# Half of the decay masks, one convolution tap and a scaling move to ScalarE in an FFN, SSD and convolution block

## The chip, the cores and the metric

The kernel runs as one program on one core of a Trainium2 chip. The metric is device time in microseconds (us). The time before is 1519.1 us, the median of three runs (1518.18 to 1520.67).

## The reference

One layer for 512 tokens of 1024 features, all in float32. Cut to what the change touches:

```python
x = x + 0.5 * swiglu(rms_norm(x, ffn1_norm), ffn1_w_in, ffn1_w_out)
h = rms_norm(x, mix_norm)
b_gate, c_gate, xa, z, xbc, dt_raw, ga, gb = split(h @ w_in)
y_a = (b_gate * causal_dwconv(c_gate * xa, short_conv_w)) @ short_w_out

xbc = silu(causal_dwconv(xbc, ssm_conv_w) + ssm_conv_b)        # 4 taps, bias
xs, bm, cm = split(xbc)                                        # 32 heads of 64; 8 groups of 128
dt = softplus(dt_raw + ssm_dt_bias);  a = -exp(ssm_A_log) * dt
decay = exp(segsum(a))               # exp of the sums of a over (s, l] within a chunk
y_diag = (C B^T * decay) @ (xs * dt) # within a chunk; y_off comes from the states before it
y_ssm = y_diag + y_off + xs * ssm_D
yf = y_ssm * silu(z)
y_b = (yf * rsqrt(mean over the group(yf^2) + eps) * ssm_norm) @ ssm_w_out

x = x + (sigmoid(ga) * y_a + sigmoid(gb) * y_b) @ w_out
x = x + 0.5 * swiglu(rms_norm(x, ffn2_norm), ffn2_w_in, ffn2_w_out)
out = rms_norm(x, final_norm)
```

## The kernel before

Features lie on the 128 partitions and the 512 tokens along the free axis. A float32 product is made of three float32r matmuls: weight and activation are each split into a high and a low part, and high times high, high times low and low times high are accumulated in one PSUM bank (L164 to L166). Each 128x1024 block of weights is loaded by SyncE (L121) into one of two `wraw` buffers, cast on ScalarE into `wh` (L125), and the rest `wl` is formed on VectorE (L126); `wh` and `wl` have three buffers each, so that a block is made ready two blocks ahead of its use.

TensorE's order is written by hand. `Order` counts ticks, a tick for every K-tile (three matmuls) of the main stream of projections; work that depends on other engines is put in so many ticks later with `sq.at`. The other engines' instructions are put in order by the scheduler of the framework, and each engine then runs its list in that order: an instruction that waits holds all behind it.

The mixer's SSD part goes over 8 groups of 4 heads, and each over 4 chunks of 128 tokens (`NC`). For a group, TensorE projects C, B and two tiles of x; each projection goes through `conv_silu`: `xp` is the scaled projection (VectorE, L372), `cv` starts as the tap of the present token (VectorE, L374), the three other taps are added (VectorE, L376), and ScalarE adds the bias and takes the SiLU (L378) into `cb` (C and B) or `xsT` (x). `inner` (L409) multiplies C and B. `x_tokens` turns x to tokens on partitions (`tr`, copied to `xt` by ScalarE, L431) and scales it into `xdd` (L437) and `xdt` (L440). For a chunk c, `steps` makes the masked decay steps `au`, two tiles of 128x512 in the high part `ah` and the low part `al` of a (GpSimd, L471), with three buffers; `weights` sums them on TensorE into the bank `sg` (two buffers, L480), ScalarE takes the exp into `ex` (L483), and VectorE masks it with `cbm` (L484); `within` (L493) multiplies by `xdt` into the bank `py`, and VectorE adds to `y` (L497, L498). `states` (L453) puts its product in the bank `po`, one buffer, which ScalarE (L458, first chunk) or VectorE (L460 and L463) reads before the next one may start. `skip` (L445) starts `y` on GpSimd. `gated` multiplies by the gate `zs`, squares and sums on ScalarE (L520), VectorE and GpSimd make the scale `rg` (L525, L527), and four VectorE instructions scale `y` (L529). `out` transposes y (L537) and ScalarE copies it to `yk` (L539). Group g's late steps run on TensorE among the projections of group g + 1, and for groups 1 to 7 the gate's products (L311 to L313) stand between the last x projection and the next group's.

Of the kernel before, what the change touches and what calls it, by code (L numbers as in the profile page):

```python
# [17 lines left out]
P = 128  # L18
# [14 lines left out]
# columns of the packed per-feature parameters  # L33
# [8 lines left out]
class Order:  # L42
    """The order of the tensor engine's work: the main stream advances in ticks (a K-tile of a
    projection each); what depends on other engines is put in so many ticks later."""
# [25 lines left out]
def hybrid_block(ctx: ExitStack, tc: tile.TileContext, xT, w1i, w1o, wmx, wz0, wso, wsso,  # L70
# [39 lines left out]
    def prep():  # L110
        """The next block of weights as two float32r parts whose sum is exact."""
# [46 lines left out]
    def mm3(out, w, xs, first=True, last=True, tk=slice(0, T)):  # L158
        """out += w.T @ x over the K-tiles xs, both in pairs of parts, for the tokens tk."""
# [19 lines left out]
    class Norm:  # L179
        """RMS norm of the residual: the parts of x * gain, and 1 / RMS per token, which the  # L180
        products are scaled by afterwards."""
# [119 lines left out]
    def gate(zw, wide, c0, cn):  # L301
        """z of a group for the token blocks c0 .. c0 + cn, tokens on the partitions."""
# [34 lines left out]
    def dt_chain():  # L337
        # softplus(v) = max(v, 0) + log1p(exp(-|v|)), log1p(e) = 2 atanh(e / (2 + e))
# [20 lines left out]
    def decays():  # L359
        """exp of the sums of a within a chunk: up to a token, after it, and of all."""  # L360
# [7 lines left out]
    def conv_silu(o, pt, ft):  # L368
        """Scale, causal convolution over 4 taps, bias and SiLU of one 128-channel tile."""
# [4 lines left out]
        nc.vector.tensor_scalar(cv, xp[:, 3:], col(PF_CW + 4 * ft + 3), None, ALU.mult)  # L374
# [3 lines left out]
        nc.scalar.activation(o, cv, AF.Silu, bias=col(PF_CB + ft))  # L378
# [7 lines left out]
    class Group:  # L386
        """One group of the SSD mixer: 4 heads that share B and C."""
# [10 lines left out]
        def heads(self, apx):  # L398
            """Values of the group's heads, each over its 64 channels."""
            n = apx.shape[1]  # L400
            return apx[:, :, self.hs].unsqueeze(3).broadcast_to([P, n, HG, HD])
# [356 lines left out]
```

## Time and profile before

| what | us |
| --- | --- |
| median of three runs | 1519.1 |
| the profiled execution: its span, first to last instruction | 1517.2 |
| around the span, by the median | 1.9 |
| TensorE busy | 1492.1 |
| VectorE busy | 830.2 |
| ScalarE busy | 533.9 |
| GpSimd busy | 267.3 |

The profiled execution has no time of its own besides its span; the 1.9 us are the median less the span. The first feed-forward runs to about 375 us, the SSD groups from there to about 760 us, then come the merge, the short convolution and the second feed-forward. A TensorE instruction's end is modelled and overlaps the next one's start, so that the start of one matmul to the start of the next tells its true cost: a projection's matmul is shown with 0.40 and the next starts 0.23 later.

### The profile page before, as it was taken

The page shows a single profiled execution, that of the slowest core. Times are in us where ns is not written, and L with a number is a line of the kernel's source. Part 1 is how long each engine was busy: PE and PEld are TensorE (multiplying, and loading weights), DVE is VectorE, ACT ScalarE, POOL GpSimd, SP SyncE. Part 2 cuts the span into 40 slices and gives each one's busy share as a digit, 9 for nine tenths or more (in the row PEclk, how much of TensorE's full clock was granted, in tenths as well). Part 3 has the DMA queues.
Part 4 walks back from the last instruction along what each step waited for, and adds up shares of the span by engine and source line. Part 5 has one row for each costly group of instructions (what it writes and reads, how often), then busy time and mean ns, then how long its engine had stood idle before and what let it go on. Part 6 is the DMA issues. An engine that isn't in the chain of part 4 may idle for free.

```text
span 1517.2 us, 17880 instructions
## 1 busy us (share of the span) xinstructions
PE 1492.1 (98%) x7214; PEld 1255.7 (83%) x7214; DVE 830.2 (55%) x990; ACT 533.9 (35%) x721; POOL 267.3 (18%) x236
## 2 busy tenths in 40 slices
PE   7999999999999999999999999999999999999997
PEld 6888888888878888888988888888888888888887
DVE  5545454323797877888754246654454545453223
ACT  5323222222455555445542122223243323232232
POOL 0111111000045442344300001111121111110011
PEclk9999999999999999999999999999999999999998
DMA  5333333323221221222222233333222222223233
GB/s 178 98 97 98 97 97 91 104 87 98 84 70 53 73 68 59 84 70 70 70 84 97 97 98 97 98 97 98 97 97 95 87 103 91 102 93 104 87 104 105
DMA packets 41539, 139.48 MB, mean 92 GB/s; under 512 B 4592, under 2 KB 7024, under 8 KB 41456
## 3 DMA queue, kind: packets, MB, share of 16 engines
q1 hardware_dynamic: 41456, 138.34, 28.7%
q8 instruction: 57, 0.93, 0.2%
q14 instruction: 26, 0.21, 0.0%
HBM read 136.22 MB, written 2.10 MB: 91 GB/s over the span
## 4 chain that ended last, share of the span: by engine, by line
PE 90%; DVE 5%; issue 3%; ACT 1%; DMA 0%; POOL 0%; SPq 0%; POOLq 0%; DVEq 0%; ACTq 0%
PE mm L166 27%; PE mm L164 27%; PE mm L165 27%; PE py L493 1%; PE mm L313 1%; PE mm L312 1%; PE mm L311 1%; DVE ex L484 1%; DVE wl L126 1%; PE po L504 1%; DVE xdd L437 1%; DVE cv L376 1%; PE sg L212 0%; ACT L483 0%; PE po L453 0%
## 5 line engine op out<-in xcount | busy, mean ns | idle before, releaser
L125 ACT CAST wh<-wraw 128x1024 fp32r<-128x1024 f32 (+3 forms) x261 | 269.6, 1033 | 715.9 <-PE mm L165 655.9
L164 PE MATMUL mm<-xw,wh 128*128 128x512 f32 x1256 | 503.2, 401 | 7.6 <-ACT wh L125 5.7
L126 DVE TENSOR_TENSOR wl<-wraw,wh 128x1024 fp32r<-128x1024 f32 (+3 forms) x261 | 394.2, 1511 | 199.7 <-ACT wh L125 198.5
L166 PE MATMUL mm<-xw,wl 128*128 128x512 f32 x1256 | 491.3, 391 | 0.3 <-DVE wl L126 0.3
L165 PE MATMUL mm<-xw,wh 128*128 128x512 f32 x1256 | 491.1, 391 | 0.0
L164 PEld LDWEIGHTS mm<-xw,wh 128*128 128x128 f32 x1256 | 237.0, 189 | 55.4 <-ACT wh L125 5.7
L166 PEld LDWEIGHTS mm<-xw,wl 128*128 128x128 f32 x1256 | 236.8, 189 | 51.6 <-DVE wl L126 1.4
L165 PEld LDWEIGHTS mm<-xw,wh 128*128 128x128 f32 x1256 | 237.2, 189 | 48.5 <-DVE xw L192 0.8
L164 PE MATMUL mm<-hk,wh 128*128 128x512 f32 (+1 forms) x374 | 141.1, 377 | 0.0
L165 PE MATMUL mm<-hk,wh 128*128 128x512 f32 (+1 forms) x374 | 140.8, 377 | 0.0
L166 PE MATMUL mm<-hk,wl 128*128 128x512 f32 (+1 forms) x374 | 140.8, 376 | 0.0
L250 POOL TENSOR_TENSOR hf<-sg,tu 128x512 f32<-128x512 f32 x44 | 58.6, 1331 | 401.9 <-ACT wh L125 343.2
L248 DVE TENSOR_TENSOR tu<-mm,rb 128x512 f32<-128x512 f32 x42 | 29.0, 691 | 134.6 <-PE mm L166 134.6
L165 PEld LDWEIGHTS mm<-hk,wh 128*128 128x128 f32 x374 | 70.4, 188 | 13.0
L164 PEld LDWEIGHTS mm<-hk,wh 128*128 128x128 f32 x374 | 70.4, 188 | 12.9
L166 PEld LDWEIGHTS mm<-hk,wl 128*128 128x128 f32 x374 | 70.4, 188 | 12.8
L376 DVE SCALAR_TENSOR_TENSOR cv<-xp,pf,cv 128x512 f32<-128x512 f32 x96 | 74.9, 780 | 1.2
L311 PE MATMUL mm<-wh,xw 128*128 128x256 f32 (+1 forms) x256 | 75.2, 294 | 0.0
L312 PE MATMUL mm<-wl,xw 128*128 128x256 f32 (+1 forms) x256 | 72.7, 284 | 0.0
L313 PE MATMUL mm<-wh,xw 128*128 128x256 f32 (+1 forms) x256 | 72.7, 284 | 0.0
L244 DVE TENSOR_TENSOR tg<-mm,rb 128x512 f32<-128x512 f32 x43 | 29.7, 691 | 67.8 <-PE mm L166 64.2
L203 POOL TENSOR_TENSOR nacc<-nacc,nsq 128x512 f32<-128x512 f32 x18 | 26.4, 1468 | 223.5 <-ACT nsq L201 223.5
(181 smaller groups left out, 1670.5 us busy)
## 6 DMA issues: line engine op xcount, KB each, us to landing
wraw<-wmx SPq DMA_DIRECT2D x86, 512.0 KB, 3.5
wraw<-w2i SPq DMA_DIRECT2D x44, 512.0 KB, 3.2
wraw<-w1i SPq DMA_DIRECT2D x43, 512.0 KB, 3.5
wraw<-w2o SPq DMA_DIRECT2D x18, 512.0 KB, 3.5
wraw<-w1o SPq DMA_DIRECT2D x16, 512.0 KB, 3.5
wraw<-wsso SPq DMA_DIRECT2D x16, 512.0 KB, 3.7
wraw<-wso SPq DMA_DIRECT2D x8, 512.0 KB, 3.2
wraw<-wmo SPq DMA_DIRECT2D x8, 512.0 KB, 3.3
```

What stands on the lines that cost most here:

```text
L125: nc.scalar.copy(wh[:, h], raw[:, h])
L126: nc.vector.tensor_tensor(wl[:, h], raw[:, h], wh[:, h].bitcast(F32), ALU.subtract)
L164: nc.tensor.matmul(out, wh[:, sl], xk[:, 0, tk], start=first and i == 0, stop=False)
L165: nc.tensor.matmul(out, wh[:, sl], xk[:, 1, tk], start=False, stop=False)
L166: nc.tensor.matmul(out, wl[:, sl], xk[:, 0, tk], start=False, stop=last and i == n - 1)
L244: nc.vector.tensor_tensor(tg, pg, nrm.rb, ALU.mult)
L248: nc.vector.tensor_tensor(tu, pu, nrm.rb, ALU.mult)
L250: nc.gpsimd.tensor_tensor(hf, sg, tu, ALU.mult)
L311: nc.tensor.matmul(o, xw[k][:, 0, tk], wh[:, sl], start=k == 0, stop=False)
L312: nc.tensor.matmul(o, xw[k][:, 0, tk], wl[:, sl], start=False, stop=False)
L313: nc.tensor.matmul(o, xw[k][:, 1, tk], wh[:, sl], start=False, stop=k == KT - 1)
L376: nc.vector.scalar_tensor_tensor(cv, xp[:, q : q + T], col(PF_CW + 4 * ft + q), cv, ALU.mult, ALU.add)
```

## The change

Four edits in the SSD part; the number of matmuls and the order of TensorE's and SyncE's instructions stay as they were.

- `steps`: the high half of the masked steps (`ah`) is no longer one GpSimd instruction of 128x512 but four ScalarE copies of 128x128, one a head, each with the head's value of a as a scale per partition. The low half stays on GpSimd.
- `conv_silu`: the first tap with the bias is a ScalarE instruction (Identity, with a scale and a bias per partition) in place of a VectorE one, and the SiLU no longer has a bias.
- `gated`: the four scalings of `y` by `rg` are ScalarE copies with a scale in place of VectorE instructions.
- Comments and docstrings are gone. Lines behind them move by at most 6: `ah` is L473, `al` L477, the exp L489, the first tap L374, the other taps L377, the SiLU L379, the scaling of `y` L535.

```diff
@@ -366,16 +366,17 @@
         nc.vector.tensor_tensor(dtd, dt, ds, ALU.mult)
 
     def conv_silu(o, pt, ft):
-        """Scale, causal convolution over 4 taps, bias and SiLU of one 128-channel tile."""
+
         xp = tp.tile([P, T + 3], F32, tag="ta", name="xp")
         nc.gpsimd.memset(xp[:, 0:3], 0.0)
         nc.vector.tensor_tensor(xp[:, 3:], pt, nm.rb, ALU.mult)
         cv = tp.tile([P, T], F32, tag="tb", name="cv")
-        nc.vector.tensor_scalar(cv, xp[:, 3:], col(PF_CW + 4 * ft + 3), None, ALU.mult)
+        nc.scalar.activation(cv, xp[:, 3:], AF.Identity, scale=col(PF_CW + 4 * ft + 3),
+                             bias=col(PF_CB + ft))
         for q in (2, 1, 0):
             nc.vector.scalar_tensor_tensor(cv, xp[:, q : q + T], col(PF_CW + 4 * ft + q), cv,
                                            ALU.mult, ALU.add)
-        nc.scalar.activation(o, cv, AF.Silu, bias=col(PF_CB + ft))
+        nc.scalar.activation(o, cv, AF.Silu)
 
     def hview(t, c0, c1):
         return t[:, c0:c1, :].rearrange("p c (h d) -> p c h d", d=HD)
...
@@ -464,17 +465,22 @@
             self.st[c + 1] = sn
 
         def steps(self, c):
-            """a of chunk c masked to the tokens up to l, [t, head, l], in two parts."""
+
             self.au[c] = []
-            for part in (ah.bitcast(F32), al):
-                au = tp.tile([P, HG, P], F32R, tag="td", name="au", bufs=3)
-                nc.gpsimd.tensor_tensor(
-                    au, tri.unsqueeze(1).broadcast_to([P, HG, P]),
-                    part[:, c, self.hs].unsqueeze(2).broadcast_to([P, HG, P]), ALU.mult)
-                self.au[c].append(au)
+            au = tp.tile([P, HG, P], F32R, tag="td", name="au", bufs=3)
+            for h in range(HG):
+                k = self.g * HG + h
+                nc.scalar.activation(au[:, h, :], tri, AF.Copy,
+                                     scale=ah.bitcast(F32)[:, c, k : k + 1])
+            self.au[c].append(au)
+            au = tp.tile([P, HG, P], F32R, tag="td", name="au", bufs=3)
+            nc.gpsimd.tensor_tensor(
+                au, tri.unsqueeze(1).broadcast_to([P, HG, P]),
+                al[:, c, self.hs].unsqueeze(2).broadcast_to([P, HG, P]), ALU.mult)
+            self.au[c].append(au)
 
         def weights(self, c):
-            """exp(sum of a over (s, l]) * C B^T of chunk c, [s, head, l]."""
+
             sgp = bank("sg")
             for i in range(2):
                 nc.tensor.matmul(sgp, mgt_r, self.au[c][i].rearrange("p h l -> p (h l)"),
...
@@ -526,8 +532,8 @@
             rg = tp.tile([P, NC], F32, tag="rg", name="rg")
             nc.gpsimd.tensor_tensor(rg, sm, nhalf, ALU.pow)
             for c in range(NC):
-                nc.vector.tensor_scalar(self.y[:, c, :], self.y[:, c, :], rg[:, c : c + 1], None,
-                                        ALU.mult)
+                nc.scalar.activation(self.y[:, c, :], self.y[:, c, :], AF.Copy,
+                                     scale=rg[:, c : c + 1])
 
         def out(self, i):
             if i == 0:
```

The scheduler puts ScalarE's, VectorE's and GpSimd's lists in another order. Three places follow. In these lists a row is a line, an operation, out<-in and a shape, `x4` stands for four in a row, and buffer numbers are left out except in the names of the states (`st_4661`).

GpSimd at the start of the mixer, group 0, from the scale `rt` of the norm on. Before:

```order
L217 TENSOR_TENSOR rt<-ms,nhalf 128x4
L371 MEMSET xp 128x3 x4
L471 TENSOR_TENSOR au<-cst,ah 128x512
L471 TENSOR_TENSOR au<-cst,al 128x512
L471 TENSOR_TENSOR au<-cst,ah 128x512
L371 MEMSET xp 128x3
L471 TENSOR_TENSOR au<-cst,al 128x512
L471 TENSOR_TENSOR au<-cst,ah 128x512
L445 TENSOR_TENSOR y<-xt,pr 128x1024
L471 TENSOR_TENSOR au<-cst,al 128x512
L471 TENSOR_TENSOR au<-cst,ah 128x512
```

The same stretch of GpSimd after:

```order
L217 TENSOR_TENSOR rt<-ms,nhalf 128x4
L371 MEMSET xp 128x3 x3
L477 TENSOR_TENSOR au<-cst,al 128x512
L371 MEMSET xp 128x3 x2
L446 TENSOR_TENSOR y<-xt,pr 128x1024
L477 TENSOR_TENSOR au<-cst,al 128x512 x3
L371 MEMSET xp 128x3 x2
L477 TENSOR_TENSOR au<-cst,al 128x512
L371 MEMSET xp 128x3
```

The `ah` tiles are gone, and `skip` (the instruction that writes `y`) and two more memsets now stand ahead of the second `al` tile, that of chunk 1; before, that tile stood ahead of `skip`.

ScalarE in a late group, from the group's first exp to the third (the same in groups 2 to 6). Before:

```order
L483 ACTIVATE ex<-sg 128x512
L431 COPY xt<-tr 128x4x128
L483 ACTIVATE ex<-sg 128x512
L125 CAST wh<-wraw 128x1024
L320 ACT_TABLE_LOAD
L320 ACTIVATE zs<-mm,rt 128x256
L458 COPY st_4661<-po 128x256
L320 ACTIVATE zs<-mm,rt 128x256
L125 CAST wh<-wraw 128x1024
L483 ACT_TABLE_LOAD
L483 ACTIVATE ex<-sg 128x512 x2
```

The same stretch of ScalarE after:

```order
L489 ACTIVATE ex<-sg 128x512
L432 COPY xt<-tr 128x4x128
L473 ACTIVATE au<-cst,ah 128x128 x4
L489 ACTIVATE ex<-sg 128x512
L473 ACTIVATE au<-cst,ah 128x128 x4
L125 CAST wh<-wraw 128x1024
L320 ACT_TABLE_LOAD
L320 ACTIVATE zs<-mm,rt 128x256
L459 COPY st_4721<-po 128x256
L320 ACTIVATE zs<-mm,rt 128x256
L125 CAST wh<-wraw 128x1024
L473 ACTIVATE au<-cst,ah 128x128 x2
```

Four `au` instructions stand behind the first exp and the copy `xt`, four behind the second exp ahead of the cast of weights, and two behind the second cast (four and two more follow behind the third exp).

VectorE in a late group around the convolution of B, from the gating of `y` on. Before:

```order
L372 TENSOR_TENSOR xp<-mm,rb 128x512
L126 TENSOR_TENSOR wl<-wraw,wh 128x1024
L374 TENSOR_SCALAR cv<-xp,pf 128x512
L525 TENSOR_SCALAR sm<-sm 128x4
L376 SCALAR_TENSOR_TENSOR cv<-xp,pf,cv 128x512
L529 TENSOR_SCALAR y<-y,rg 128x256
L376 SCALAR_TENSOR_TENSOR cv<-xp,pf,cv 128x512
L529 TENSOR_SCALAR y<-y,rg 128x256
L376 SCALAR_TENSOR_TENSOR cv<-xp,pf,cv 128x512
L529 TENSOR_SCALAR y<-y,rg 128x256 x2
```

The same stretch of VectorE after:

```order
L521 TENSOR_TENSOR y<-y,zs 128x512
L372 TENSOR_TENSOR xp<-mm,rb 128x512
L126 TENSOR_TENSOR wl<-wraw,wh 128x1024
L531 TENSOR_SCALAR sm<-sm 128x4
L377 SCALAR_TENSOR_TENSOR cv<-xp,pf,cv 128x512 x3
L372 TENSOR_TENSOR xp<-mm,rb 128x512
```

The first tap (L374) and the scalings of `y` (L529) are gone from between the taps. They stand on ScalarE, in the same group:

```order
L526 ACTIVATE jk,sm<-y 128x256 x2
L374 ACTIVATE cv<-xp,pf 128x512
L535 ACTIVATE y<-y,rg 128x256 x4
L379 ACTIVATE cb<-cv 128x512
L125 CAST wh<-wraw 128x1024
```

The tap of B stands behind the squares `jk`, then the four scalings, which wait for `rg`, and behind them the SiLU of B (`cb`).

## Rows read from the trace of the kernel before

**Rows 1.** The page's first part: busy us, share of the span, instructions of each engine.

```profile
PE 1492.1 (98%) x7214; PEld 1255.7 (83%) x7214; DVE 830.2 (55%) x990; ACT 533.9 (35%) x721; POOL 267.3 (18%) x236
```

**Rows 2.** Waits of TensorE in the mixer: total us, times, longest.

```profile
PE po L453 <- DVE st L463: 3.5, 5, 0.7
PE po L453 <- DVE xdd L437: 1.9, 1, 1.9
PE sg L409 <- ACT ex L483: 1.5, 1, 1.5
PE sg L480 <- POOL au L471: 1.3, 1, 1.3
PE po L453 <- ACT st L458: 0.5, 1, 0.5
```

**Rows 3.** Timeline, TensorE, group 2: start, us, instruction, [idle before <-releaser].

```profile
520.68 0.40 PE L166 MATMUL mm<-xw,wl 128*128 128x512 f32 x1
521.76 0.70 PE L453 MATMUL po<-xdd,btk 128*128 128x256 f32 x2 [0.69 <-DVE st L463]
```

**Rows 4.** Windows: stretch, length; PE, PEld, DVE, ACT, POOL busy; PEclk, DMA share, GB/s.

```profile
521.00:566.00 45.00, 44.31 (x271) 39.66 (x271) 37.00 (x54) 22.57 (x36) 17.98 (x17) 1.00 0.23 69
440.00:443.00 3.00, 2.30 (x11) 2.31 (x12) 3.00 (x4) 1.91 (x3) 0.63 (x1) 0.62 0.00 0
467.00:472.00 5.00, 4.48 (x14) 3.64 (x15) 5.00 (x5) 2.97 (x4) 3.25 (x2) 0.66 0.01 3
```

**Rows 5.** Groups by form: busy us, mean ns of one, idle before.

```profile
L471 POOL TENSOR_TENSOR au<-cst,ah 128x512 fp32r<-128x512 f32 x32 | 44.0, 1374 | 1.3 <-DVE ah L356 1.3
L374 DVE TENSOR_SCALAR cv<-xp,pf 128x512 f32<-128x512 f32 x32 | 17.9, 558 | 0.7
L529 DVE TENSOR_SCALAR y<-y,rg 128x256 f32<-128x256 f32 x32 | 11.7, 396 | 7.7 <-POOL rg L527 7.7
L378 ACT ACTIVATE cb<-cv,pf 128x512 f32<-128x512 f32 x16 | 11.6, 724 | 36.8 <-DVE cv L376 36.8
L320 ACT ACTIVATE zs<-mm,rt 128x256 f32<-128x256 f32 x32 | 14.4, 475 | 5.0 <-PE mm L313 5.0
```

**Rows 6.** Timeline, VectorE, group 2, ahead of the wait of rows 3.

```profile
514.91 2.91 DVE L126 TENSOR_TENSOR wl<-wraw,wh 128x1024 fp32r<-128x1024 f32 x1
...
518.92 2.06 DVE L126 TENSOR_TENSOR wl<-wraw,wh 128x1024 fp32r<-128x1024 f32 x1
...
521.30 0.41 DVE L463 TENSOR_TENSOR st<-po,st 128x256 f32<-128x256 f32 x1
```

**Rows 7.** Timeline, GpSimd, the same stretch.

```profile
514.40 2.34 POOL L445 TENSOR_TENSOR y<-xt,pr 128x1024 f32<-128x1024 f32 x1
```

**Rows 8.** Timeline, ScalarE, the same stretch: the two casts.

```profile
512.90 1.05 ACT L125 CAST wh<-wraw 128x1024 fp32r<-128x1024 f32 x1 [0.88 <-PE mm L313]
...
516.26 1.07 ACT L125 CAST wh<-wraw 128x1024 fp32r<-128x1024 f32 x1
```

**Rows 9.** Timeline, GpSimd, VectorE, TensorE, mixer's start, group 0.

```profile
424.76 1.04 POOL L471 TENSOR_TENSOR au<-cst,al 128x512 fp32r<-128x512 f32 x1
...
427.48 2.87 POOL L445 TENSOR_TENSOR y<-xt,pr 128x1024 f32<-128x1024 f32 x1
...
428.52 0.68 DVE L372 TENSOR_TENSOR xp<-mm,rb 128x512 f32<-128x512 f32 x1
...
426.70 0.62 PE L480 MATMUL sg<-au,mgt_r 128*128 128x512 f32 x2
...
429.94 0.39 PE L480 MATMUL sg<-au,mgt_r 128*128 128x512 f32 x1
431.58 0.50 PE L480 MATMUL sg<-au,mgt_r 128*128 128x512 f32 x1 [1.26 <-POOL au L471]
```

**Rows 10.** Timeline, VectorE, GpSimd, ScalarE, TensorE, group 3: B's convolution and `inner`.

```profile
534.80 1.22 DVE L126 TENSOR_TENSOR wl<-wraw,wh 128x1024 fp32r<-128x1024 f32 x1
...
536.58 1.51 POOL L527 TENSOR_TENSOR rg<-sm,nhalf 128x4 f32<-128x4 f32 x1 [3.54 <-DVE sm L525]
...
540.09 0.72 ACT L378 ACTIVATE cb<-cv,pf 128x512 f32<-128x512 f32 x1 [0.42 <-DVE cv L376]
...
541.36 1.05 PE L409 MATMUL sg<-cb 128*128 128x128 f32 x8
```

## The prediction

> **What bounds the kernel now.** The page comes first: TensorE is busy for 1492.1 us, 98% of the span of 1517.2 us, the other engines for 55% or less [rows 1]. The change leaves TensorE's instructions and their order as they are, so it can give back only what TensorE loses, and only in the SSD part, where the four edits are. The waits of TensorE come next [rows 2]: five kinds, 8.7 us together. 3.5 us of it is one wait that recurs in five groups: the state product L453 waits for `po`, which L463 on VectorE has still to read. The other 5.2 us are single waits of groups 0 and 1. Then the timeline: such a wait is dearer than its idle time. In group 2 the matmul before starts at 520.68, the next one would follow 0.23 later and follows 1.08 later: 0.85 lost, where 0.69 is shown as idle [rows 3]. Five of these are 4.3 us. The single waits cost 5.2 + 5 x 0.16 = 6.0 us by the same surcharge (five waits). Last, the clock: the waits of 1.5 and 1.9 us at 440 and 467 are followed by a granted clock of 1.2 instead of 2.4 GHz, and the stretches around them stand at means of 0.62 over 3 us and 0.66 over 5 us [rows 4], which is 0.38 x 3 + 0.34 x 5 = 2.8 us of missing clock. The wait of 1.26 at 431.58 [rows 9] and the five of 0.69 have no such mark: the stretch with one of them has clock 1.00 [rows 4]. **The most there is to win** is 4.3 + 6.0 + 2.8 = 13.1 us, 0.9%.
>
> **What the edits cost on their engines.** Away go 4 high halves of masks a group from GpSimd, 4 x 1.37 = 5.5 us, and from VectorE 4 taps and 4 scalings, 4 x 0.56 + 4 x 0.40 = 3.8 us a group [rows 5]. On ScalarE 16 copies of 128x128, 4 taps of 128x512 and 4 scalings of 128x256 are added per group. Rows of before show no 128x128 with a scale; from 0.475 at 256 columns and 0.724 at 512 (both with a value per partition) the line goes to 0.35 at 128 [rows 5]. Bounds are 0.25, if neighbours overlap by a tenth, and 0.475, the nearest row itself; I take 0.30, so four take 1.2 (1.0 to 1.9) and sixteen 4.8. A tap is the 0.724 of the SiLU that also takes a value per partition, or somewhat more for its second one: 0.75, four 3.0. Scalings are 4 x 0.40 = 1.6 (1.5 to 1.9). Sum 9.4 us a group. ScalarE is busy for 22.6 of 45.0 us in such a group [rows 4]; 32 of 45 is 71%, so its rate does not become the bound. The table loads are as many as before by the lists of the two programs. SyncE's DMAs and their order stay; the weight casts stand two blocks ahead of their use and cover a delay of some us.
>
> A rule speaks against this change: the Trainium skill, page "ScalarE: Activation LUTs", section "Rules for kernel authors", gives multiplications and additions to VectorE rather than ScalarE. Its price is an estimate of 0.39 us for a 128-column copy with one pointer operand, of which about 0.09 overlaps with a neighbour: sixteen take 4.7 us, and the sum stays. The row agrees that the tap is dearer on ScalarE (0.72 against 0.56 us), but what counts here is who is late for TensorE.
>
> **The five recurring waits (groups 2 to 6).** VectorE's order ahead of L463 stays: two rests of weights, 2.91 and 2.06 us long, and then L463 at 521.30, done at 521.71 [rows 6]; TensorE wanted it at 520.68 + 0.23 = 520.91. It is late by 0.8. A rest of weights takes 1.22 where GpSimd has little to do [rows 10]; here GpSimd runs `skip` from 514.40 for 2.34 us [rows 7] and masks on either side, and the two are 2.5 us longer than two times 1.22. With the high halves gone, GpSimd starts `skip` sooner by up to one mask (1.4) and has one low half left in the stretch, so half of the 2.5 us should go: L463 ends at about 520.4, half a us early. Against it stands ScalarE: eight copies, 2.4 us, come ahead of the cast of 512.90, which now sits behind 0.88 of idle time [rows 8], with as much again ahead of the second exp. The casts get later by some 0.3 to 0.9, so the second ends at about 517.33 + 0.9 = 518.2, and the rest at 518.92 [rows 6] still finds it done. If it holds, the whole 4.3 goes; what is late next is the pair of copies behind the second cast, which delays the third exp; the code puts its TensorE use 11 ticks behind the sums, 11 x 3 x 0.23 = 7.6 us. I book -4.3 (bounds 0 and -4.3).
>
> By the Trainium skill, page "SBUF — State Buffer", section "Who interferes with whom", a VectorE operation with two SBUF inputs and a GpSimd operation that reads SBUF exclude each other for the whole instruction. By this L463 gains only what GpSimd really frees, one mask and the earlier start of `skip`, and the margin of half a us is all there is. The pairs in rows 6 and 7 agree: 2.91 is 1.2 and most of the 2.34 of `skip`.
>
> **Groups 0 and 1.** Here the rows show waits on four engines, and the change moves all four; I walk the list.
> Chunk 1 of group 0: its low half is written at 424.76 to 425.80 and TensorE uses it from 426.70 [rows 9]. After, `skip` stands ahead of it on GpSimd. `skip` starts where that half starts now, less the 0.56 of a tap of C that is gone from VectorE: about 424.2, takes 2.3 to 2.9 [rows 7, 9], and the half another 1.0: 427.5 to 428.1, say 427.7, against 426.70 + 0.23 a new wait of 0.7 (0 to 2).
> Chunk 2: now 1.26 late for its low half [rows 9]. After, its high half comes from ScalarE, behind the first tap of group 1's B, which waits for `xp` on VectorE at 428.52 to 429.20 [rows 9], then a tap 0.7, a cast 1.05 and four copies 1.2: 432.2, against a use at 429.94 + 0.7 = 430.6. A wait of about 1.5 (0.5 to 2.5) for one of 1.3: together these two lose 2.2 where now 1.4 are lost.
> The waits for the state copy (0.5), for the exp at 440 (1.5 with its slow clock) should go: on ScalarE both stand behind the SiLU of group 1's B, whose taps VectorE ends sooner with one tap less and less of GpSimd beside it. The wait for `xdd` (1.9 with its slow clock) ends sooner, since the scalings of y no longer stand ahead of `xdd` on VectorE and GpSimd has two masks less; I keep 0.6 of it, and 1.5 for the states' transfers and for the copies of group 1's chunk 2, for which no row of before gives a price (bounds 0 and 1.9, the longest wait here).
> Left: 2.2 + 0.6 + 1.5 = 4.3 of 6.0, and the clock's 2.8 go if no wait exceeds about 1.4, of which the 1.5 of chunk 2 is the doubtful one. -1.7 - 2.8 = -4.5 (bounds -8.8, all gone, and +1.7, as much as now and one more slow spell).
>
> **Sum.** -4.3 - 4.5 = -8.8 us. Against the span of 1517.2: 1508.4. With 1.9 around it, 1510.3 against the median of 1519.1: 0.6% faster. A change within 0.2%, about 3.0 us, can't be told from none. Bounds: 1519.1 - 13.1 = 1506.0, and 1519.1 + 1.7 = 1520.8 with no new recurring wait.
>
> **Rivals.**
> *L463 stays late.* If the casts are later than I count, or the masks that are left meet the two rests, the five waits stay. For it: the order ahead of L463 is unchanged. Against it: 2.5 us of lengthening for 0.8 of lateness. Time 1519.1 - 4.5 = 1514.6.
> *The start gives nothing back.* The new waits at chunks 1 and 2 and a slow spell after them eat what the others free. For it: `skip` ahead of a low half, a high half behind a tap. Time 1519.1 - 4.3 = 1514.8.
> *Both*: the waits only change their names; 1519 +/- 2, no change. This is also the case in which the change doesn't do what it says: VectorE and GpSimd are relieved, TensorE sees nothing of it.
> *ScalarE becomes late for B, slower than before.* `cb` of B is done at 540.09 + 0.72 = 540.81 and TensorE takes it at 541.36: 0.55 in hand [rows 10]. After, the SiLU stands behind the four scalings, and these behind `rg`, which GpSimd ends at 536.58 + 1.51 = 538.09 [rows 10]. 538.1 + 1.6 + 0.72 = 540.4: 0.95 in hand. From one us more on ScalarE or GpSimd on, every one of seven groups waits; with waits of 1.5 and a slow spell of 1.7 each that is 7 x 3.2 = 22 us, and 1510.3 + 22 = 1532. For it: tap, scalings and SiLU are now one queue. Against it: `rg` should come no later, and VectorE's taps sooner, as they no longer wait for it.
>
> **How the numbers follow.** The forecast has 0.60 (its own range 1507 to 1513.5). L463 stays late 0.13, the start gives nothing 0.10, both 0.09, ScalarE late for B 0.08. Faster by over 0.2% are the first three, 0.83; same 0.09; slower 0.08. A range for 8 in 10 takes in the forecast and the two middle cases: 1506.5 to 1516.
>
> **What would show it.** Right: no wait of L453 for VectorE's L464 (the former L463) in groups 2 to 6, GpSimd busy 44 us less, ScalarE some 70 us more, TensorE's clock at 1.00 around 440. Step by step: the low half of chunk 1 ending near 427.7; a copy of the masks near 0.30 each. Wrong: a TensorE wait that recurs per group for `cb`, `au` or an exp, or copies of 0.45 or more, which would put the casts behind VectorE's need.

## The result and the profile after

The changed kernel takes 1505.5 us (median of four runs, 1505.25 to 1506.23); the kernel before 1518.6 us (1516.52 to 1520.67, four runs, three of them those of the 1519.1 that the forecast set out from). The ratio is 0.991, with a 95% interval of 0.990 to 0.992: faster by 0.9%. The forecast was 1510.3 with a range of 1506.5 to 1516.0. The direction is as forecast, and so is the mechanism of the five recurring waits; the gain is half as large again, and the time lies 1.0 us under the range. The step that failed is the start of the mixer (groups 0 and 1), which was booked at 4.5 us and gave 7.4.

The page's first part of the changed kernel, in the columns of [rows 1], and the waits of TensorE that are left in the mixer, in those of [rows 2]:

```profile
PE 1486.7 (99%) x7214; PEld 1254.1 (83%) x7214; DVE 795.4 (53%) x926; ACT 604.6 (40%) x913; POOL 219.9 (15%) x204
```

```profile
PE sg L486 <- ACT au L473: 1.4, 1, 1.4
PE po L510 <- DVE yo L513: 0.5, 1, 0.5
PE sg L486 <- POOL au L477: 0.2, 1, 0.2
```

GpSimd is busy for 47.4 us less and ScalarE for 70.7 us more, and the span went from 1517.2 to 1504.5. Of the five recurring waits of L453 (now L454) for the state sum none is left, and none of the single waits for `xdd`, for the exp and for the state copy. Chunk 2 of group 0 now waits 1.4 us for its high half, which comes from ScalarE, where it waited 1.3 for its low half from GpSimd. The wait for `yo` (0.5) was 0.15 before, and the one of 0.2 for chunk 1's low half was none. The clock tells the rest. Windows of the changed kernel (columns as in [rows 4]) over the stretch in which the kernel before has its two spells at 1.2 GHz:

```profile
430.00:440.00 10.00, 8.55 (x48) 7.07 (x46) 9.42 (x14) 9.92 (x18) 2.66 (x4) 1.00 0.17 52
440.00:445.00 5.00, 5.00 (x32) 4.44 (x31) 4.09 (x8) 4.96 (x9) 0.24 (x1) 1.00 0.37 108
460.00:470.00 10.00, 10.00 (x59) 8.66 (x58) 10.00 (x11) 9.94 (x21) 5.59 (x3) 1.00 0.19 54
470.00:480.00 10.00, 10.00 (x58) 8.73 (x57) 7.61 (x15) 7.01 (x15) 2.02 (x3) 1.00 0.35 105
```

The granted clock is 1.00 in all four, and TensorE is busy throughout three of them. For the kernel before the second of these windows is

```profile
440.00:445.00 5.00, 4.01 (x16) 3.42 (x17) 5.00 (x9) 2.64 (x4) 0.73 (x2) 0.66 0.31 89
```

The two traces hold the same 7214 matmuls in the same order, so that the start of each can be laid beside its twin, and the lead of the changed kernel (by how much sooner in its span the twin starts) read off step by step. The lead is 0.17 when the mixer begins. Over group 0's chunks 1 and 2 it falls by 0.7. It grows by 0.8 where the wait for the state copy was, by 1.6 where the exp at 440 was waited for and by 1.7 in the slow spell behind that, by 0.6 where `py` was waited for (0.3 idle, too short for [rows 2]), falls by 0.4 at the wait for `yo`, and grows by 2.1 where `xdd` was waited for and by 1.6 in the second slow spell: it then stands at 7.53, which is 7.36 us for the start. Then it grows by 0.96 at each of five state products, 0.86 at the product that waited and 0.10 at the one right behind it, and by some hundredths in between: 4.95 us for the five groups. With 0.23 in the rest of the span it is 12.71.

How the state sum (L463, now L464) got on time is seen in group 2. Timeline of the changed kernel, VectorE from `xdd` to that sum, then GpSimd in the same stretch (start, us, instruction):

```profile
503.08 0.95 DVE L438 TENSOR_TENSOR xdd<-xt,dtd 128x768 f32<-128x768 f32 x1
503.94 2.06 DVE L441 TENSOR_TENSOR xdt<-xt,dt 128x1024 f32<-128x1024 f32 x1
505.93 2.38 DVE L490 TENSOR_TENSOR ex<-ex,cbm 128x512 f32<-128x512 f32 x1
508.23 2.06 DVE L126 TENSOR_TENSOR wl<-wraw,wh 128x1024 fp32r<-128x1024 f32 x1
510.21 0.41 DVE L461 TENSOR_TENSOR st<-st,dec 128x256 f32<-128x256 f32 x1
510.55 1.21 DVE L126 TENSOR_TENSOR wl<-wraw,wh 128x1024 fp32r<-128x1024 f32 x1
...
512.08 0.41 DVE L464 TENSOR_TENSOR st<-po,st 128x256 f32<-128x256 f32 x1
```

```profile
503.72 1.21 POOL L477 TENSOR_TENSOR au<-cst,al 128x512 fp32r<-128x512 f32 x1 [2.72 <-PE sg L486]
504.89 2.87 POOL L446 TENSOR_TENSOR y<-xt,pr 128x1024 f32<-128x1024 f32 x1
507.72 1.49 POOL L477 TENSOR_TENSOR au<-cst,al 128x512 fp32r<-128x512 f32 x1
```

What counts is the ends. `xdt` ends at 506.00, 1.07 behind the mask that ended at 504.93; `ex` ends at 508.31, 0.55 behind the `y` that ended at 507.76; the first rest of weights `wl` ends at 510.29, 1.08 behind the mask that ended at 509.21. The second `wl`, with GpSimd at rest, takes 1.21. The two engines take turns: a VectorE operation on two SBUF tiles that meets a GpSimd product runs nearly its whole length (1.07 of 1.22, 0.55 of 0.69) after that product's end, and the other way round (`y` ends 1.76 behind the end of `xdt`). Three products are met on the way. From the start of `xdd` to the end of the state sum the changed kernel needs 512.49 - 503.08 = 9.41 us.

In the kernel before that stretch is 521.71 - 510.61 = 11.10 us, and VectorE is not idle in it. Its rows beyond [rows 6, 7], VectorE and then GpSimd:

```profile
510.61 0.95 DVE L437 TENSOR_TENSOR xdd<-xt,dtd 128x768 f32<-128x768 f32 x1
511.48 2.06 DVE L440 TENSOR_TENSOR xdt<-xt,dt 128x1024 f32<-128x1024 f32 x1
513.46 1.52 DVE L484 TENSOR_TENSOR ex<-ex,cbm 128x512 f32<-128x512 f32 x1
...
517.74 1.26 DVE L460 TENSOR_TENSOR st<-st,dec 128x256 f32<-128x256 f32 x1
```

```profile
511.25 1.21 POOL L471 TENSOR_TENSOR au<-cst,al 128x512 fp32r<-128x512 f32 x1 [1.72 <-PE sg L480]
512.42 2.02 POOL L471 TENSOR_TENSOR au<-cst,ah 128x512 fp32r<-128x512 f32 x1
...
516.70 2.02 POOL L471 TENSOR_TENSOR au<-cst,al 128x512 fp32r<-128x512 f32 x1
518.68 1.22 POOL L471 TENSOR_TENSOR au<-cst,ah 128x512 fp32r<-128x512 f32 x1
```

Each of `xdt`, `ex`, `wl`, `st` and `wl` meets one product here, and each is longer than the same operation by itself (1.22 in the run junk_write below, 0.69, 1.21, 0.41, 1.21), by 0.84, 0.83, 1.70, 0.85 and 0.85: 5.07 us. In the changed kernel it is 0.84, 1.69 and 0.85: 3.38 us. The difference, 1.69, is that of the two stretches: two products fewer, the high halves, at 0.85 each.

### The profile page after: what moved, and what is told of

The parts are those of the page before. It is cut to its first block, busy times and chain, and to the rows that moved or that the text cites. A ratio compares the mean times of both kernels' runs of the same rounds, so it can differ in the third digit from the quotient of the medians.

```text
span 1504.5 us, 17996 instructions
## 1 busy us (share of the span) xinstructions
PE 1486.7 (99%) x7214; PEld 1254.1 (83%) x7214; DVE 795.4 (53%) x926; ACT 604.6 (40%) x913; POOL 219.9 (15%) x204
## 4 chain that ended last, share of the span: by engine, by line
PE 96%; DVE 2%; DMA 1%; issue 1%; ACT 0%; SPq 0%; POOL 0%; POOLq 0%; ACTq 0%; DVEq 0%
PE mm L164 28%; PE mm L165 28%; PE mm L166 27%; PE mm L312 2%; PE mm L311 2%; PE mm L313 2%; PE py L499 2%; PE sg L486 1%; DVE cv L377 1%; PE po L510 1%; PE po L454 1%; DVE wl L126 0%; PE sg L212 0%; PE sg L410 0%; PE tr L431 0%
## 5 line engine op out<-in xcount | busy, mean ns | idle before, releaser
L126 DVE TENSOR_TENSOR wl<-wraw,wh 128x1024 fp32r<-128x1024 f32 (+3 forms) x261 | 386.6, 1482 | 206.8 <-ACT wh L125 205.6
L377 DVE SCALAR_TENSOR_TENSOR cv<-xp,pf,cv 128x512 f32<-128x512 f32 x96 | 73.8, 769 | 2.6 <-ACT cv L374 1.1
```

The costliest lines, as they stand in the source:

```text
L126: nc.vector.tensor_tensor(wl[:, h], raw[:, h], wh[:, h].bitcast(F32), ALU.subtract)
L377: nc.vector.scalar_tensor_tensor(cv, xp[:, q : q + T], col(PF_CW + 4 * ft + q), cv, ALU.mult, ALU.add)
```

## Experiments: which of the edits did it

Six kernels take the change apart. Each piece is one of the three pieces of the diff shown ahead of the prediction.

**The masks alone** (label masks_only).

```diff
-            for part in (ah.bitcast(F32), al):
...
+            for h in range(HG):
+                k = self.g * HG + h
+                nc.scalar.activation(au[:, h, :], tri, AF.Copy,
+                                     scale=ah.bitcast(F32)[:, c, k : k + 1])
```

> Only the high masks go to ScalarE; taps and scalings of y stay on VectorE. Theory G (GpSimd's high masks and VectorE's operations hold each other up, and that lengthens the two rests of weights ahead of L463): the five waits of 0.69 us for L463 in groups 2 to 6 go without the other two edits, 4.8 us from 1518.6; with a share of the start (the waits for the low half and for xdd) 1509 to 1514. Theory V (VectorE's own work, 8 operations a group, was what was too much): the five waits stay, 1516 to 1519.

Measured: 1506.95 us (1506.4 to 1508.17), ratio 0.992 (0.991 to 0.994). That is 2 us under the range expected. The five state waits are gone. The masks alone give 12.2 us against the kernel before beside them, where the whole change gives 13.1.

**The taps alone** (taps_only).

```diff
-        nc.vector.tensor_scalar(cv, xp[:, 3:], col(PF_CW + 4 * ft + 3), None, ALU.mult)
+        nc.scalar.activation(cv, xp[:, 3:], AF.Identity, scale=col(PF_CW + 4 * ft + 3),
+                             bias=col(PF_CB + ft))
...
-        nc.scalar.activation(o, cv, AF.Silu, bias=col(PF_CB + ft))
+        nc.scalar.activation(o, cv, AF.Silu)
```

> Only the first tap with its bias goes to ScalarE. Theory G: the five waits stay at about 0.7 us each; at the start the wait of 1.46 us for the exp at 440, behind the taps of B, shrinks: 1515 to 1518. Theory V: the five waits shrink by half or go, 1512 to 1516.

Measured: 1518.72 us, ratio 0.9996 (0.9986 to 1.0006). The five state waits stand unchanged, as does the wait for `xdd`; the one for the exp, which was to shrink, is 2.2 where it was 1.5.

**The scalings alone** (scale_only).

```diff
-                nc.vector.tensor_scalar(self.y[:, c, :], self.y[:, c, :], rg[:, c : c + 1], None,
-                                        ALU.mult)
+                nc.scalar.activation(self.y[:, c, :], self.y[:, c, :], AF.Copy,
+                                     scale=rg[:, c : c + 1])
```

> Only the scaling of y goes to ScalarE. Theory G: the five waits stay; the wait for xdd at 467 (1.92 us and 1.7 us of slow clock after it) goes or shrinks below 1, as VectorE no longer scales y ahead of it: 1514 to 1517. Theory V: the five waits go too, 1510 to 1513.

Measured: 1519.13 us, ratio 1.0004 (0.9995 to 1.0014): the five waits stay, but the gain that was expected of the wait for `xdd` did not come. TensorE's waits in the mixer and two windows of this kernel:

```profile
PE po L453 <- DVE st L463: 6.1, 6, 2.7
PE py L493 <- DVE y L498: 1.9, 1, 1.9
```

```profile
440.00:445.00 5.00, 2.86 (x20) 2.42 (x21) 5.00 (x9) 2.18 (x3) 0.27 (x2) 1.00 0.34 105
470.00:480.00 10.00, 7.31 (x41) 5.97 (x40) 8.08 (x13) 3.40 (x6) 3.00 (x3) 1.00 0.37 106
```

The wait for `xdd` in group 1 is gone, and the same loss has moved on: the state sum of that group is now 2.7 late, at 475, and `py` at 444 is 1.9 late. VectorE's timeline ahead of it:

```profile
464.86 2.91 DVE L440 TENSOR_TENSOR xdt<-xt,dt 128x1024 f32<-128x1024 f32 x1
467.70 2.06 DVE L126 TENSOR_TENSOR wl<-wraw,wh 128x1024 fp32r<-128x1024 f32 x1
469.68 1.52 DVE L484 TENSOR_TENSOR ex<-ex,cbm 128x512 f32<-128x512 f32 x1
471.12 1.26 DVE L460 TENSOR_TENSOR st<-st,dec 128x256 f32<-128x256 f32 x1
```

Each of the four is longer than by itself (1.22, 1.21, 0.69, 0.41): they take turns with `skip` and the masks, which are all still on GpSimd.

**Taps and scalings together** (no_masks; the pieces of `conv_silu` and `gated`, the masks as before).

```diff
-        nc.vector.tensor_scalar(cv, xp[:, 3:], col(PF_CW + 4 * ft + 3), None, ALU.mult)
+        nc.scalar.activation(cv, xp[:, 3:], AF.Identity, scale=col(PF_CW + 4 * ft + 3),
+                             bias=col(PF_CB + ft))
...
-        nc.scalar.activation(o, cv, AF.Silu, bias=col(PF_CB + ft))
+        nc.scalar.activation(o, cv, AF.Silu)
...
-                nc.vector.tensor_scalar(self.y[:, c, :], self.y[:, c, :], rg[:, c : c + 1], None,
-                                        ALU.mult)
+                nc.scalar.activation(self.y[:, c, :], self.y[:, c, :], AF.Copy,
+                                     scale=rg[:, c : c + 1])
```

> Taps and scalings on ScalarE, the high masks stay on GpSimd. Theory G: the five waits of L453 for the state sum are there as before (about 0.7 us each, VectorE's two rests of weights 4.5 to 5 us together), the start gains: 1510 to 1515. Theory V: the five waits are gone, 1505 to 1508 as with the whole change.

Measured: 1520.09 us, ratio 1.0005 (0.9995 to 1.0014); the start did not gain as expected. The state sum is waited for six times, up to 2.7. VectorE is busy for 810.1 us, 20.1 us less than before, and that gives nothing as long as GpSimd multiplies the high halves.

**Masks and scalings** (no_taps) and **masks and taps** (no_scale). Against the changed kernel, the first takes the tap back:

```diff
-        nc.scalar.activation(cv, xp[:, 3:], AF.Identity, scale=col(PF_CW + 4 * ft + 3),
-                             bias=col(PF_CB + ft))
+        nc.vector.tensor_scalar(cv, xp[:, 3:], col(PF_CW + 4 * ft + 3), None, ALU.mult)
...
-        nc.scalar.activation(o, cv, AF.Silu)
+        nc.scalar.activation(o, cv, AF.Silu, bias=col(PF_CB + ft))
```

and the second the scalings:

```diff
-                nc.scalar.activation(self.y[:, c, :], self.y[:, c, :], AF.Copy,
-                                     scale=rg[:, c : c + 1])
+                nc.vector.tensor_scalar(self.y[:, c, :], self.y[:, c, :], rg[:, c : c + 1], None,
+                                        ALU.mult)
```

> Masks and scalings on ScalarE, taps on VectorE as before. The masks alone gave 1506.95, all three edits 1505.54. If the scalings bring the last 1.4 us, this gives 1505.5 with no wait of 0.7 for y and none of 0.9 for yo; if the taps bring it, 1507. The new wait of 1.4 us for the high half of group 0's chunk 2, behind the tap of group 1's B, should be gone here in either case (0.2 or none).

> Masks and taps on ScalarE, scalings on VectorE as before. If the taps bring the last 1.4 us beyond the masks, 1505.5; if the scalings do, 1507, with the masks-alone waits for y and yo (0.7 and 0.9) in place. The wait of 1.4 us of group 0's chunk 2 for its high half should be there, since the tap stands ahead of the copies as in the whole change.

Measured: 1506.8 us (1505.65 to 1508.28) and 1506.4 us (1505.86 to 1506.85); ratios 0.992 (0.991 to 0.994) and 0.992 (0.991 to 0.994). Neither time can be told from the other, nor surely from the masks alone. The waits do tell: without the taps the wait of 1.4 for chunk 2's high half is not there, and waits for `y` (0.7), `yo` (0.9) and the exp (0.6) are; with the taps it is there (1.4 and 1.5) whether or not the scalings are. The intervals of masks alone and of the whole change (0.990 to 0.992) overlap, so that the times don't show that the other two edits give anything. In the traces, one execution each, the lead over the kernel before grows by 4.95 in the five groups of every kernel with the masks, and at the start by 6.15 with the masks alone, 6.69 with the taps too, 7.04 with the scalings instead and 7.36 with all three: if they are worth something, each brings a part. The expectation that one of them would bring it all found no support.

## Experiments: why the masks did it

Two theories say why high halves on GpSimd cost TensorE time. By the first the products take turns with VectorE and so make the state sum late. By the second GpSimd itself is late.

**Unused products put back** (junk_read): GpSimd multiplies the high half into the tile of the low half, which it then overwrites. VectorE's and ScalarE's lists are those of the changed kernel.

```diff
+            nc.gpsimd.tensor_tensor(
+                au, tri.unsqueeze(1).broadcast_to([P, HG, P]),
+                ah.bitcast(F32)[:, c, self.hs].unsqueeze(2).broadcast_to([P, HG, P]), ALU.mult)
             nc.gpsimd.tensor_tensor(
...
```

> The whole change, but GpSimd still makes each high half too, into the tile that it then overwrites with the low half: GpSimd's work is that of before, ScalarE's and VectorE's lists are those of the changed kernel, instruction for instruction. Theory G (GpSimd's reads beside VectorE's): the five waits for the state sum come back at 0.5 to 0.9 us and VectorE's two rests of weights ahead of it take 4.3 to 5 us together; 1510 to 1514. Rival D (what counted is only that the high half is no longer made late by GpSimd, a dependency): the five waits stay away, each low half is 1 to 2 us later, so waits for it at the start alone: 1506 to 1509.

**Unused fills put in** (junk_write): in the same place two fills with zeros.

```diff
+            nc.gpsimd.memset(au.bitcast(F32), 0.0)
+            nc.gpsimd.memset(au.bitcast(F32), 0.0)
             nc.gpsimd.tensor_tensor(
...
```

> The whole change, and GpSimd fills each low-half tile twice with zeros before it makes it: GpSimd is busy and late again, but with instructions that read nothing. Theory G, in the form that only two readers exclude each other: VectorE's two rests of weights keep 3.3 us together, the five waits stay away, 1505 to 1508. Rival B (any GpSimd instruction beside VectorE's lengthens these): the rests take over 4 us, the waits come back, 1509 to 1514.

Measured: 1528.7 us (1527.71 to 1529.77) and 1532.0 us (1526.93 to 1536.44), ratios 1.006 (1.004 to 1.007) and 1.008 (1.005 to 1.010): both slower than the kernel before, and both outside all that was expected. Neither does what it was made for. The wait that took over, in the first and in the second:

```profile
PE sg L489 <- POOL au L480: 16.6, 7, 2.9
```

```profile
PE sg L488 <- POOL au L479: 19.7, 8, 2.9
```

The unused work stands ahead of the low half (in group 2 `skip` comes between the two as well), and TensorE then waits for the low half itself, 2.3 us in each of groups 2 to 7 of the first. A late low half hides the state sum behind it, so the two theories can't be told apart here. What the pair shows is that GpSimd's list ahead of the low half of chunk 2 has no room for another product or two fills with each mask.

**The products taken from the kernel before** (mem_high): here nothing is moved to ScalarE. In the kernel before, the high half is left out of the result, and GpSimd fills that tile twice with zeros instead. That takes GpSimd as long as an undisturbed product (0.53 + 0.53 against 1.04), and all other lists are those of the kernel before (in GpSimd's own list `skip` comes one fill sooner).

```diff
-                nc.gpsimd.tensor_tensor(
-                    au, tri.unsqueeze(1).broadcast_to([P, HG, P]),
-                    part[:, c, self.hs].unsqueeze(2).broadcast_to([P, HG, P]), ALU.mult)
+                if part is not al:
+                    nc.gpsimd.memset(au.bitcast(F32), 0.0)
+                    nc.gpsimd.memset(au.bitcast(F32), 0.0)
+                else:
+                    nc.gpsimd.tensor_tensor(
+                        au, tri.unsqueeze(1).broadcast_to([P, HG, P]),
+                        part[:, c, self.hs].unsqueeze(2).broadcast_to([P, HG, P]), ALU.mult)
```

> The kernel before, in which each high half of the masks is left out: GpSimd fills that tile twice with zeros instead of multiplying. Two fills take 1.05 us (0.52 and 0.53 in the run with two fills ahead of each low half), a product beside an idle VectorE 1.04, so GpSimd's list is as long as before, and VectorE's, ScalarE's and TensorE's lists are those of the kernel before. Lock theory: a VectorE operation on two SBUF tiles and a GpSimd product take turns, so that each product met costs VectorE about 0.85 us, and a fill costs it nothing. Then the stretch of VectorE from xdd to the end of L463's successor in group 2 shortens from 11.1 us to 9.4 or less (in the changed kernel 9.4), the five waits for the state sum go, and the time is that of the masks alone, 1505.5 to 1508.5. Rival: what the high halves cost is GpSimd's own time (a late low half, a late skip); then the five waits of 0.7 stay, and the time is 1517 to 1520.5.

Measured: 1507.7 us (1507.41 to 1508.22), ratio 0.993 (0.992 to 0.994). The five state waits are gone. Timeline of this kernel in group 2, VectorE and GpSimd:

```profile
505.39 0.95 DVE L437 TENSOR_TENSOR xdd<-xt,dtd 128x768 f32<-128x768 f32 x1
506.26 2.06 DVE L440 TENSOR_TENSOR xdt<-xt,dt 128x1024 f32<-128x1024 f32 x1
508.25 2.38 DVE L488 TENSOR_TENSOR ex<-ex,cbm 128x512 f32<-128x512 f32 x1
510.55 2.08 DVE L126 TENSOR_TENSOR wl<-wraw,wh 128x1024 fp32r<-128x1024 f32 x1
...
512.88 1.21 DVE L126 TENSOR_TENSOR wl<-wraw,wh 128x1024 fp32r<-128x1024 f32 x1
...
514.41 0.41 DVE L463 TENSOR_TENSOR st<-po,st 128x256 f32<-128x256 f32 x1
```

```profile
510.51 1.04 POOL L475 TENSOR_TENSOR au<-cst,al 128x512 fp32r<-128x512 f32 x1
511.49 0.53 POOL L472 MEMSET au<- 128x512 f32 x1
512.08 0.52 POOL L473 MEMSET au<- 128x512 f32 x1
```

From `xdd` to the end of the state sum: 514.82 - 505.39 = 9.43 us, the 9.4 that the turns gave. The first `wl` ends 1.08 behind the low half that ended at 511.55, and two fills run beside it without making it longer. The fills also let GpSimd go on sooner: the second low half here starts 4.47 behind the first (506.04), in the kernel before 5.45 (511.25 to 516.70). But VectorE is not idle in either stretch, so that what made its state sum late were its own lengthened operations. The five waits thus come from GpSimd's products shutting out VectorE, not from the time that GpSimd spends or from ScalarE's part in the change. This agrees with the Trainium skill, page "SBUF — State Buffer", section "Who interferes with whom": a VectorE instruction with two SBUF inputs contends with a GpSimd instruction that reads SBUF, not with one that only writes it.

## Experiments: how close the slower case was

The rival that ended slower had ScalarE late for B, from one microsecond more on. GpSimd's making of `rg`, which the scalings and then the SiLU of B wait for, is done twice (rg2, the diff) and three times (rg3, with `range(3)`).

```diff
-            nc.gpsimd.tensor_tensor(rg, sm, nhalf, ALU.pow)
+            for _ in range(2):
+                nc.gpsimd.tensor_tensor(rg, sm, nhalf, ALU.pow)
```

> The whole change with the scale of y made twice on GpSimd, so that the scalings and B's SiLU behind them on ScalarE come 1.0 to 1.5 us later; all lists keep their order. The profile of the changed kernel has this SiLU done 1.65 us before TensorE takes it: if ScalarE's queue there has this slack, no wait appears and the time stays at 1505 to 1507. If the slack is used up by something else, seven waits of up to 1 us: 1508 to 1514.

> The same with the scale made three times, 2.1 to 3.0 us later. By the slack of 1.65 us each of groups 1 to 7 waits 0.5 to 1.4 us for B's SiLU: 1509 to 1516, and slow clock behind the waits would come on top. If the scalings aren't on the path to that SiLU: 1505 to 1507.

Measured: 1506.8 us (1506.46 to 1507.4) for two and 1515.1 us (1513.94 to 1515.89) for three. TensorE's waits for `cb`, first of rg2 and then of rg3:

```profile
PE sg L410 <- ACT cb L379: 0.5, 1, 0.5
```

```profile
PE sg L410 <- ACT cb L379: 6.0, 6, 1.6
```

The chain is real, and its margin is that of the changed kernel's trace in group 3 (ScalarE, TensorE):

```profile
528.98 1.71 ACT L535 ACTIVATE y<-y,rg 128x256 f32<-128x256 f32 x4 [1.70 <-POOL rg L533]
530.60 0.62 ACT L379 ACTIVATE cb<-cv 128x512 f32<-128x512 f32 x1
```

```profile
532.86 0.83 PE L410 MATMUL sg<-cb 128*128 128x128 f32 x6
```

`cb` is done at 531.22 and used at 532.86: 1.64 us in hand. One more `rg` of 1.4 to 1.5 us nearly fits, two do not: five of the six waits of rg3 are 0.88.

**The tap of group 1's B back on VectorE** (b1_tap), a try at the one new wait of 1.4 us.

```diff
-        nc.scalar.activation(cv, xp[:, 3:], AF.Identity, scale=col(PF_CW + 4 * ft + 3),
-                             bias=col(PF_CB + ft))
+        if ft == 17:
+            nc.vector.tensor_scalar(cv, xp[:, 3:], col(PF_CW + 4 * ft + 3), col(PF_CB + ft),
+                                    ALU.mult, ALU.add)
+        else:
+            nc.scalar.activation(cv, xp[:, 3:], AF.Identity, scale=col(PF_CW + 4 * ft + 3),
+                                 bias=col(PF_CB + ft))
```

> The whole change, but the tap of group 1's B stays on VectorE. That tap stands on ScalarE ahead of the high half of group 0's chunk 2, for which TensorE waits 1.4 us, the longest wait left in the mixer. Theory: ScalarE need not wait for xp there, the copies come about 2 us sooner, the wait goes, 1505.5 - 1.4 = 1504.1. Rival: the wait is taken over by the next one in the line (the exp of that chunk, or the low half), and the time stays at 1505.5 within 0.5.

Measured: 1505.9 us (1504.44 to 1506.49), not to be told from the changed kernel, as the rival had it. The wait is gone, and in its place TensorE waits for the exp of group 0 and longer for `yo`:

```profile
PE sg L414 <- ACT ex L493: 1.0, 1, 1.0
PE po L514 <- DVE yo L517: 0.7, 1, 0.7
```

No kernel here is clearly faster than the changed one; its waits left in the mixer are 2.1 us together.

## Why the prediction was right in kind and too small in size

**The five recurring waits: right, 4.95 us where 4.3 were booked.** The step that about half of the 2.5 us of lengthening would go gave the state sum at 520.4; laid on the clock of before (the lead is 7.5 us there) it ends at 520.0, 0.9 ahead of its use. The better rule was in the sentence on taking turns: two products fewer are met, 2 x 0.85 us. The term is short by 0.10 a wait, as the second of the two state matmuls behind a wait also starts 0.10 later, which [rows 3] folds into one row of x2.

**The start: the term that was mis-sized, 7.4 us where 4.5 were booked.** Its parts:

- Chunks 1 and 2 were to lose 0.8 more than before and lose 0.7 more. The new wait for chunk 1's low half is 0.2 where 0.7 were booked, and this is in part luck: `skip` started at 423.49 and not at 424.2, and took 1.90 and not 2.3 to 2.9, but the low half behind it met `xdd` on VectorE and took 1.75 where 1.0 was booked, so that it ended at 427.10 and not at 427.7. Chunk 2's wait is 1.4 where 1.5 were booked. In the trace this high half is made as the prediction had it: tap behind `xp`, cast, four copies.

```profile
428.87 0.82 ACT L374 ACTIVATE cv<-xp,pf 128x512 f32<-128x512 f32 x1 [2.28 <-DVE xp L372]
429.60 1.03 ACT L125 CAST wh<-wraw 128x1024 fp32r<-128x1024 f32 x1
430.53 1.27 ACT L473 ACTIVATE au<-cst,ah 128x128 fp32r<-128x128 f32 x4
```

- 1.5 us were kept for waits that no row priced (the states' transfers, group 1's copies). Of these came 0.4, at `yo`. That is 1.1 of the 2.9 missing.
- 0.6 us were kept of the wait for `xdd`, and nothing of it stayed.
- The wait for `py` (0.3 idle, 0.6 in the lead) was not on the list of [rows 2] and went too. (The surcharge of 0.16 was counted for five single waits, where the list has four; that is 0.2 too much in the 6.0.)
- The clock gave back 3.3 us where 2.8 were booked. The first stretch of [rows 4] ends before its spell does: over 440 to 445 the mean clock is 0.66, and 0.34 x 5 = 1.7 us where 1.1 were counted. The condition put beside this term, no wait above about 1.4, did not hold up as a rule: see the last section.

**The rest of the miss, 1.3 us:** 0.4 of the lead lie outside the start and the five groups, and 0.9 is the distance of median and span, 1.9 for the kernel before and 1.0 for the changed one. Of that 0.7 is spread between executions: the profiled one of the changed kernel is the slowest of its four, 1506.2, with 1.7 around its span. The bound of all waits gone, 1506.0, was in the text, and the range stopped 0.5 above it; the result is 0.5 under it.

**What each edit costs on its engine: right.** Four copies of the masks take 1.27 to 1.29 us in a row (forecast 1.2), six 1.86, so 0.31 each (0.30); four scalings 1.71 (1.6). The tap is dearer than booked:

```profile
L374 ACT ACTIVATE cv<-xp,pf 128x512 f32<-128x512 f32 x32 | 26.0, 814 | 6.7 <-DVE xp L372 6.6
```

0.81 against 0.75. ScalarE is busy for 32.2 of 45 us in the stretch that answers to 521 to 566, as forecast (32). Nothing of it reaches TensorE, but for chunk 2 of group 0.

**What the edits are worth: wrong in what the prediction gave to two of them.** It booked the start partly to taps and scalings leaving VectorE. The runs show these two alone at nothing, singly and together. In mem_high, where neither edit is made, the lead over the kernel before grows by 5.75 us at the start, where the changed kernel's grows by 7.36: most of the start too came from products that met VectorE's operations. There the turns had made GpSimd late as well: of the 5.75, 1.4 are the wait for chunk 2's low half, ahead of which the kernel before has a high half of 1.76 us (425.76) and a `y` of 2.87, mem_high a fill of 0.52 (426.07) and a `y` of 2.40. In mem_high, waits of 1.4 for the exp, 1.1 for `py` and 1.0 for `xdd` stay, which the whole change does not have. The rule of the page "ScalarE: Activation LUTs" in the Trainium skill, section "Rules for kernel authors", that multiplications belong on VectorE, holds for the duration of the tap (0.81 against 0.56 us); for the masks it would have kept off the ScalarE list the only edit that gains.

**The rivals.** The state sum did not stay late; the start gave more, not nothing; ScalarE was not late for B: `rg` ended at 528.94, which on the clock of before is 537.4, 0.7 sooner than [rows 10], and so the margin became 1.64 where 0.95 were worked out.

## What to carry to other kernels

A GpSimd product that reads SBUF costs twice: its own time and a turn taken from any VectorE operation on two SBUF tiles that it meets. Where a VectorE operation on the path is longer than its twin elsewhere by about the rest of a GpSimd instruction, count how many products are met on the way to the late instruction; moving one of them to ScalarE, or, for such operations, making it a pure write, is worth a whole turn (0.85 us here), while taking other work off VectorE may be worth nothing. Before booking a reserve for waits that no row shows, ask which of the shown waits share the cause that the change removes: here most did, and they went together.

## What the runs showed of the hardware

The turns are exact to some hundredths of a microsecond: `xdt` and `wl` end 1.07 to 1.08 us behind the product that they met, `ex` 0.55, in the changed kernel and in mem_high alike. In the kernel before 75 of the 77 rests of weights of 128x1024 that overlap a GpSimd product end 1.08 or 1.09 behind one. VectorE operations that take one input from PSUM are not held: the state sum takes 0.41 in all three kernels, beside a mask too.

An operation with a single input tile, from SBUF to SBUF, is held as well, and a fill holds it too. The tap on VectorE takes 0.48 us alone; in the kernel before one takes 1.40, from 429.23, and ends 0.28 behind the `y` of [rows 9]. In mem_high one takes 1.86, from 427.84, and ends 0.28 behind a fill (428.90, 0.52 long), and a scaling of `y` that takes 0.35 elsewhere takes 0.69 beside a fill (458.56). So a pure write frees VectorE's operations on two SBUF tiles, but not these.

A wait's length alone did not decide on the slow clock. A wait of 1.5 us at 440 and one of 1.9 at 467 are followed by spells at 1.2 GHz in the kernel before [rows 4]. In scale_only the twin of the first, 1.5 us at 440, is not, and neither are its waits of 1.9 at 444 and 2.7 at 475 (granted clock 1.00 in the windows shown above), nor is the one of 1.4 in the changed kernel. In junk_read the same wait of 2.29 us for the low half comes in groups 2 to 7, and two of the six are followed by a spell. Windows of this kernel behind the first and the third:

```profile
512.70:520.70 8.00, 7.99 (x40) 6.80 (x41) 5.56 (x9) 5.90 (x13) 5.54 (x4) 1.00 0.45 132
606.70:614.70 8.00, 7.94 (x32) 6.57 (x33) 4.58 (x8) 5.49 (x12) 4.22 (x4) 0.79 0.42 132
```

What else decides was not tried.

The spells do not come in every execution, either. Of 43 executions of the kernel before that were timed beside the experiments, 26 have a mean granted clock of 0.995, as the profiled one with both spells, and 12 one of 0.998, as three of the four of the changed kernel; their medians are 1520.1 and 1517.7 us. So the 3.3 us of clock are those of the two traces compared, and the changed kernel is some 12 us faster than the executions at 0.998, too. Nor is a spell's price simply added to that of the waits: in scale_only TensorE gains 1.4 us on the kernel before where the first spell is missing, and loses 1.6 at its next wait, for `py`.
